# A two-layer trunk on one core: the opening's order on VectorE written anew up to the fourth k-tile, and two rows of set 2 given to TensorE

## The chip, the core and the metric

The kernel runs on one core of one Trainium2 chip. The metric is device time in microseconds (us) of one execution; lower is better. Times are medians of several runs. The profile is of one execution of its own.

## The reference

The input is x (512 rows of 2048, float32) and a conditioning vector c (2048). Two layers follow each other; each has its own modulation by c. What matters here is only the beginning of the first layer:

```python
c_act = jax.nn.silu(c)
mod = c_act @ w_mod[l] + b_mod[l]
shift, scale, gate = jnp.split(mod, 3, axis=-1)
h = x * (1.0 + scale[:, None]) + shift[:, None]
proj = h @ w_in            # q, k, v and a gate of the first layer's attention
```

So no product `h @ w_in` can begin before a part of shift and scale is known, and each of these is a product of c_act with a 2048 x 2048 part of w_mod. After that come differential attention, an output product, a layer norm, a shared key/value product, forgetting attention, a second output product and a last layer norm.

## The kernel before

**Precision.** Every large product is done as three TensorE products (lines 174 to 176): each operand is split into a high part (`whi`, `hh`) and a low remainder (`wlo`, `hl`). A weights' split is a copy on ScalarE (L94, `whi`) and a subtraction on VectorE (L95, `wlo`). A split step loads two k-tiles of a job; the first job of a head is 384 wide, the second 512 (768 and 1024 numbers per partition).

**The opening** (from L439) works in k-tiles of 128 of the 2048 model columns. For k-tile `kt` it needs:

- the *set* that holds the k-tile's shift and scale. Sets 0 and 1 hold one k-tile each, the others two (set 2 holds k-tiles 2 and 3). A set is summed over 16 rows (pieces of 128 of the reduction). A row is one VectorE instruction: the first row writes `sacc` (L496), the 15 others add to it (L498). The pieces arrive as tiles `sms` (L471), in a ring of 5 buffers (`NBUF`);
- the *sums* of the set (`mod_sums`, L512): TensorE multiplies `sacc` with a column of ones (L528) into the bank `tr`. For set 1 TensorE also takes the last 8 of the 16 rows by itself, straight from `sms` and the column of c_act (L525, `on_pe`, L449);
- the *columns* (`mod_columns`, L531; `mcol` on VectorE, L534): the sums plus the bias;
- the *turn* (`turn_x`, L536): four transposes of x on TensorE (L539) into the same bank `tr`, of which there is one buffer; two ScalarE instructions read it with the columns, `hh` (L543) and `htmp` (L544);
- the *lower h* (`lower_h`, L548, `hl` on VectorE), which needs `htmp`;
- the *products* of the k-tile (`first_products`): 21 matmuls (7 accumulators, three products each) of 128x512 into the banks `sc` (2), `o` (1) and `acc` (4).

Products run in phases for two heads u: head 0 with k-tiles 0 to 3, then head 1 with 0 to 7, head 0 with 4 to 11, and so on. After head 0's fourth k-tile the accumulators are copied out by ScalarE (`part`, L576).

**What sets the order.** The string `START` (L31) is the order in which these steps are recorded: `c` sums, `m` columns, `t` turn, `l` lower h, `s` the next weights' split, `g` the products of the next k-tile, and a digit n for n rows of `sacc` (`dv`). Within `with tc.manual_schedule(engines={ET.DVE})` VectorE's queue stands exactly in that order; the queues of TensorE and ScalarE are ordered by a scheduler when the program is built. `sums()` first empties the set (`dv(-1)`). The rows come from a generator (`mod_steps`), which yields after it has recorded a row; so when `dv(-1)` stops, the first row of the next set has already been recorded, ahead of the columns of the set just summed.

Of the kernel before, what the change touches and what calls it, by code (L numbers as in the profile page):

```python
# [10 lines left out]
F32 = mybir.dt.float32  # L11
# [5 lines left out]
P = 128  # L17
D = 2048
KT = D // P
# [8 lines left out]
ET = mybir.EngineType  # L28


START = "cmtlssg6c6t1lgcst4g3tsl9sggts8sl6s2gtggts7lgsstlgg2s7gstl2ss9gsgtslgg5stgg6lsstg2gss8sggt2g4l4sgstctslggtslssggssgggg"  # L31
LAM_INIT = 0.8 - 0.6 * math.exp(-0.0)


# [76 lines left out]
def tile_yoco(  # L111
# [44 lines left out]
    def acc_bank(name="acc"):  # L156
        return ps.tile([P, 512], F32, name=name, tag="acc", bufs=4)
# [281 lines left out]
    with tc.tile_pool(name="start", bufs=2, reuse_waits="tile") as sp, tc.manual_schedule(engines={ET.DVE}):  # L439
# [7 lines left out]
            nc.sync.dma_start(xts[q][:, :, f0:f1], src.rearrange("(b p) f -> p b f", p=P))  # L447

        def on_pe(i):  # L449
            return 8 if i == 1 else 0  # L450


        tiles = []
# [8 lines left out]
        def load_mods(upto):  # L462
            while state["next"] < min(upto, len(tiles)):
                i, k, nr = tiles[state["next"]]
                k0, nk = sets[i]
                t = sp.tile([P, nr, 2, nk * P], F32, name="sms", tag="sms", bufs=NBUF)
                step = nr // 2 if i < 2 else nr
                for kq in range(0, nr, step):
                    for v in range(2):
                        rows = w_mod[0, (k + kq) * P : (k + kq + step) * P, v * D + k0 * P : v * D + (k0 + nk) * P]  # L470
                        nc.sync.dma_start(t[:, kq : kq + step, v, :], rows.rearrange("(k p) n -> p k n", p=P))  # L471
                loaded[i, k] = t
                state["next"] += 1
                if k == 0:
                    if k0 == 0:
                        load_x(0, 0, P)
                    elif k0 == 1:
                        load_x(0, P, T)
                    elif k0 % 4 == 0:
                        load_x(k0 // 4, 0, T)  # L480

        accs = {}

        def mod_steps():
            for n, (i, k, nr) in enumerate(tiles):
                k0, nk = sets[i]
                load_mods(n + NBUF)
                if k >= KT - on_pe(i):
                    continue
                if k == 0:  # L490
                    accs[i] = sp.tile([P, 2, 2 * P], F32, name="sacc", tag="sacc", bufs=2)
                acc = accs[i][:, :, : nk * P]
                for kq in range(nr):
                    w, sc = loaded[i, k][:, kq, :, :], cact[:, k + kq : k + kq + 1]
                    if k + kq == 0:
                        V.tensor_scalar(acc, w, sc, None, op0=ALU.mult)  # L496
                    else:
                        V.scalar_tensor_tensor(acc, w, sc, acc, op0=ALU.mult, op1=ALU.add)  # L498
                    yield i

        load_mods(2)
        ws.load(2)
        steps = mod_steps()
        ahead = [next(steps)]

# [6 lines left out]
        def mod_sums(i):  # L512
            k0, nk = sets[i]
            nr = 8 // nk
            dv(-1)
            state["set"] = i + 1
            load_mods(max(n for n, t in enumerate(tiles) if t[0] == i) + 1)
            pm = tr_bank()
            for v in range(2):
                for j in range(nk):  # L520
                    js = slice(j * P, (j + 1) * P)
                    dst = pm[:, nk * v + j : nk * v + j + 1]
                    for k in range(KT - on_pe(i), KT):
                        kr = k // nr * nr
                        PE.matmul(  # L525
                            dst, loaded[i, kr][:, k - kr, v, js], cact[:, k : k + 1], start=k == KT - on_pe(i), stop=False
                        )
                    PE.matmul(dst, accs[i][:, v, js], ones[:, 0:1], start=on_pe(i) == 0, stop=True)  # L528
            return pm
# [20 lines left out]
        acc = {}  # L550
# [71 lines left out]

        for tok in START:
            if tok.isdigit():
# [473 lines left out]
    acc = [acc_bank() for _ in range(TB)]  # L1098
# [313 lines left out]
```

## Time and profile before

| what | us |
|---|---|
| median of 3 runs (1977.61 to 1982.32) | 1979.31 |
| the profiled execution's own time | 1977.16 |
| its span on the core | 1975.4 |
| TensorE matmul busy | 1938.9 |
| VectorE busy | 1342.1 |
| ScalarE busy | 704.8 |
| first product of the opening (L174) | 18.17 |
| first product of k-tiles 1, 2 and 3 | 33.05, 43.52, 50.24 |

A row of the timeline gives start, duration, engine, line, operation, output <- inputs, shapes and count; in square brackets stands the idle time of the engine just before it and what ended it. A row of the waits gives total, number and longest. A row of the windows gives, for a stretch, the busy time of each engine, then the granted TensorE clock (1.00 is full), the share of the DMA engines and GB/s. One fp32 matmul of one column (L525, L528) stands as two records.

### The profile page before, as it was taken

The page shows a single profiled execution, that of the slowest core. Times are in us where ns is not written, and L with a number is a line of the kernel's source. Part 1 is how long each engine was busy: PE and PEld are TensorE (multiplying, and loading weights), DVE is VectorE, ACT ScalarE, POOL GpSimd, SP SyncE. Part 2 cuts the span into 40 slices and gives each one's busy share as a digit, 9 for nine tenths or more (in the row PEclk, how much of TensorE's full clock was granted, in tenths as well). Part 3 has the DMA queues.
Part 4 walks back from the last instruction along what each step waited for, and adds up shares of the span by engine and source line. Part 5 has one row for each costly group of instructions (what it writes and reads, how often), then busy time and mean ns, then how long its engine had stood idle before and what let it go on. Part 6 is the DMA issues. An engine that isn't in the chain of part 4 may idle for free.

```text
span 1975.4 us, 25112 instructions
## 1 busy us (share of the span) xinstructions
PE 1938.9 (98%) x8939; PEld 1605.5 (81%) x8939; DVE 1342.1 (68%) x2460; ACT 704.8 (36%) x1217; POOL 2.2 (0%) x10
## 2 busy tenths in 40 slices
PE   5999999999999999999999999999999999999997
PEld 4888888888888888788888888888888888888886
DVE  7885677778777777863475665666466666676657
ACT  2432445333333334431264222224343443453123
POOL 0000000000000000000000000000000000000000
PEclk8999999999999999999999999999999999999999
DMA  9993444676667666553345765664355555553622
GB/s 343 355 310 106 134 149 152 192 223 194 221 193 223 198 219 216 195 159 98 115 160 182 267 232 183 222 221 144 102 152 151 155 156 153 148 173 114 229 90 107
DMA packets 299354, 362.21 MB, mean 183 GB/s; under 512 B 44598, under 2 KB 201932, under 8 KB 298460
## 3 DMA queue, kind: packets, MB, share of 16 engines
q1 hardware_dynamic: 296848, 356.39, 56.4%
q10 hardware_dynamic: 2380, 4.21, 0.6%
q8 instruction: 70, 1.15, 0.2%
q14 instruction: 56, 0.46, 0.1%
HBM read 338.68 MB, written 21.84 MB: 183 GB/s over the span
## 4 chain that ended last, share of the span: by engine, by line
PE 93%; DVE 3%; DMA 2%; SPq 1%; issue 0%; ACT 0%; DVEq 0%; ACTq 0%
PE acc L174 27%; PE acc L175 27%; PE acc L176 27%; PE sc L174 2%; PE sc L175 2%; PE sc L176 2%; PE o L174 1%; PE o L175 1%; PE o L176 1%; DVE wlo L95 1%; SPq L471 0%; PE tr L742 0%; PE tr L789 0%; PE tr L539 0%; DMA nr<-n_dram 0%
## 5 line engine op out<-in xcount | busy, mean ns | idle before, releaser
L95 DVE TENSOR_TENSOR wlo<-wst,whi 128x1024 fp32r<-128x1024 f32 (+2 forms) x322 | 384.3, 1195 | 332.6 <-ACT whi L94 323.2
L94 ACT CAST whi<-wst 128x1024 fp32r<-128x1024 f32 (+2 forms) x322 | 331.7, 1031 | 693.4 <-PE acc L176 345.4
L174 PE MATMUL acc<-whi,hh 128*128 128x512 f32 x1232 | 484.1, 396 | 2.3 <-DVE sg L695 1.2
L175 PE MATMUL acc<-wlo,hh 128*128 128x512 f32 x1232 | 480.8, 390 | 0.1
L176 PE MATMUL acc<-whi,hl 128*128 128x512 f32 x1232 | 480.4, 390 | 0.0
L174 PE MATMUL acc<-hh,whi 128*128 128x512 f32 x1184 | 465.5, 393 | 0.1
L175 PE MATMUL acc<-hl,whi 128*128 128x512 f32 x1184 | 461.9, 390 | 0.0
L176 PE MATMUL acc<-hh,wlo 128*128 128x512 f32 x1184 | 460.8, 390 | 0.0
L174 PEld LDWEIGHTS acc<-whi,hh 128*128 128x128 f32 x1232 | 232.4, 189 | 49.0 <-DVE ztmp L926 1.5
L176 PEld LDWEIGHTS acc<-whi,hl 128*128 128x128 f32 x1232 | 231.3, 188 | 49.5
L175 PEld LDWEIGHTS acc<-wlo,hh 128*128 128x128 f32 x1232 | 231.6, 188 | 45.3 <-DVE wlo L95 0.6
L176 PEld LDWEIGHTS acc<-hh,wlo 128*128 128x128 f32 x1184 | 222.3, 188 | 47.7
L174 PEld LDWEIGHTS acc<-hh,whi 128*128 128x128 f32 x1184 | 222.5, 188 | 44.0 <-issue 1.4
L175 PEld LDWEIGHTS acc<-hl,whi 128*128 128x128 f32 x1184 | 222.6, 188 | 41.7
L391 DVE SCALAR_TENSOR_TENSOR macc<-ms,cact,macc 128x512 f32<-128x512 f32 x300 | 224.2, 747 | 36.0 <-DMA ms<-in_kv_w_mod_dram 21.4
L498 DVE SCALAR_TENSOR_TENSOR sacc<-sms,cact,sacc 128x512 f32<-128x512 f32 (+1 forms) x127 | 89.5, 705 | 5.3 <-DMA sms<-in_w_mod_dram 1.6
L725 ACT ACTIVATE e<-e,mn 128x128 f32<-128x128 f32 (+3 forms) x64 | 36.0, 563 | 121.0 <-DVE mn L721 120.8
L1218 ACT ACTIVATE eb<-eb,mnb 128x128 f32<-128x128 f32 (+1 forms) x64 | 36.0, 563 | 88.7 <-DVE mnb L1215 88.5
L1215 DVE CUSTOM_DVE_ANT_0 eb<-sc,biasb 128x128 f32<-128x128 f32 (+1 forms) x64 | 31.0, 485 | 22.1 <-PE sc L176 21.4
L391 DVE SCALAR_TENSOR_TENSOR macc<-msk,cact,macc 128x512 f32<-128x512 f32 x60 | 45.0, 750 | 1.4
L721 DVE CUSTOM_DVE_ANT_0 e<-sc,bias 128x128 f32<-128x128 f32 (+3 forms) x64 | 31.0, 485 | 16.4 <-PE sc L176 16.4
L791 ACT ACTIVATE ogT<-tr,subg 128x128 f32<-128x128 f32 x64 | 20.0, 363 | 46.1 <-PE tr L789 46.0
(263 smaller groups left out, 1768.6 us busy)
## 6 DMA issues: line engine op xcount, KB each, us to landing
wst<-in_a_w_in_dram SPq DMA_DIRECT2D x240, 256.0 KB, 3.8
ms<-in_w_mod_dram SPq DMA_DIRECT2D x64, 512.0 KB, 4.4
ms<-in_kv_w_mod_dram SPq DMA_DIRECT2D x64, 512.0 KB, 4.3
wst<-in_kv_w_dram SPq DMA_DIRECT2D x64, 512.0 KB, 3.8
wst<-in_b_w_in_dram SPq DMA_DIRECT2D x128, 256.0 KB, 3.0
sms<-in_w_mod_dram SPq DMA_DIRECT2D x56, 512.0 KB, 6.8
wst<-in_a_w_out_dram SPq DMA_DIRECT2D x32, 512.0 KB, 3.7
msk<-in_w_mod_dram SPq DMA_DIRECT2D x64, 256.0 KB, 5.6
```

What stands on the lines that cost most here:

```text
L94: self.nc.scalar.copy(hi[:, :, :w], st[:, :, :w])
L95: self.nc.vector.tensor_tensor(lo[:, :, :w], st[:, :, :w], hi[:, :, :w].bitcast(F32), op=ALU.subtract)
L174: PE.matmul(dst, lhs[0], rhs[0], start=start, stop=False)
L175: PE.matmul(dst, lhs[0], rhs[1], start=False, stop=False)
L176: PE.matmul(dst, lhs[1], rhs[0], start=False, stop=stop)
L391: ins = V.scalar_tensor_tensor(acc, w, cact[:, kt : kt + 1], acc, op0=ALU.mult, op1=ALU.add)
L498: V.scalar_tensor_tensor(acc, w, sc, acc, op0=ALU.mult, op1=ALU.add)
L721: V.tensor_tensor_reduce(out=e[:, :w], in0=sc[:, :w], in1=st["bias"][:, (3 - i) * P :], scale=-1.0, scalar=3.0e38, op0=ALU.add, op1=ALU.mi ...
L725: S.activation(e[:, :w], e[:, :w], AF.Exp, bias=mn, scale=-1.0, accum_out=rs)
L791: S.activation(ogT[2 * h + e][:, i * P : (i + 1) * P], pt[:, e * P : (e + 1) * P], AF.Copy, scale=subg[:, e : e + 1])
L1215: V.tensor_tensor_reduce(out=e[:, :w], in0=sc[:, :w], in1=bias[:, :w], scale=-1.0, scalar=3.0e38, op0=ALU.add, op1=ALU.min, accum_out=mn)
L1218: S.activation(e[:, :w], e[:, :w], AF.Exp, bias=mn, scale=-1.0, accum_out=rs)
```

## The change

Four things change, all in the opening.

1. `START` is written anew up to the fourth k-tile.
2. `mod_steps` yields before it records a row instead of after it. `dv(-1)` then stops ahead of the next set's first row, and the columns of a set are recorded ahead of that row, in all sets.
3. TensorE takes 2 rows of set 2 (L526 in the changed file, one line later than before), VectorE 14 instead of 16.
4. Through the new string one weights' split (768 numbers) stands ahead of the last rows of set 2 instead of behind them.

```diff
-START = "cmtlssg6c6t1lgcst4g3tsl9sggts8sl6s2gtggts7lgsstlgg2s7gstl2ss9gsgt...
+START = "cmt4lssgc4t3lsgcmt2lgtls9s5ggts8sl6s2gtggts7lgsstlgg2s7gstl2ss9gsgt...
```

```diff
         def on_pe(i):
-            return 8 if i == 1 else 0
+            return {1: 8, 2: 2}.get(i, 0)
...
                 load_mods(n + NBUF)
-                if k >= KT - on_pe(i):
-                    continue
-                if k == 0:
-                    accs[i] = sp.tile([P, 2, 2 * P], F32, name="sacc", tag="sacc", bufs=2)
-                acc = accs[i][:, :, : nk * P]
                 for kq in range(nr):
+                    if k + kq >= KT - on_pe(i):
+                        break
+
+                    yield i
+                    if k + kq == 0:
+                        accs[i] = sp.tile([P, 2, 2 * P], F32, name="sacc", tag="sacc", bufs=2)
+                    acc = accs[i][:, :, : nk * P]
                     w, sc = loaded[i, k][:, kq, :, :], cact[:, k + kq : k + kq + 1]
...
                         V.scalar_tensor_tensor(acc, w, sc, acc, op0=ALU.mult, op1=ALU.add)
-                    yield i
```

The rest of both strings is the same. Up to the fourth k-tile the changed program's queues, as built, stand so (names as in the profile; `x` counts equal instructions):

```
VectorE, after the 16 rows of set 0:
mcol | 4 rows of set 1 | hl (kt 0) | wlo 768 | wlo 1024 | 4 rows of set 1
4 rows of set 2 | mcol | 3 rows | hl (kt 1) | wlo 768 | 7 rows of set 2
mcol | 2 rows of set 3 | hl (kt 2) | wlo 1024 | hl (kt 3) | wlo 768
9 rows of set 3 | wlo 1024 | 5 rows of set 3 | mcol | wlo 768 | 8 rows of set 4 | wlo 1024 | hl

TensorE, from the 21 products of kt 1 on:
L526 tr<-cact,sms x2 | L529 tr<-ones,sacc      (four times)
L540 tr<-ident,xt x4 (kt 2) | 7 products of hh and whi (kt 2)
L540 tr<-ident,xt x1 (kt 3) | the other 14 products of kt 2
L540 tr<-ident,xt x3 (kt 3) | 21 products of kt 3
```

In the program before, all four transposes of kt 3 stand between the 7 and the 14 products of kt 2. ScalarE's queue has `hh` and `htmp` of kt 1 ahead of the weights' copy (L94) that stood ahead of them. On SyncE the first 43 transfers of the opening keep their order; behind them a pair of weights' loads moves ahead of six `sms` transfers. GpSimd's queue is unchanged. From the last products of the opening on, the order on TensorE is that of before, instruction for instruction.

More of the change, by code (lines that the diff above doesn't have):

```diff
@@ L28 @@
 ET = mybir.EngineType
-START = "cmtlssg6c6t1lgcst4g3tsl9sggts8sl6s2gtggts7lgsstlgg2s7gstl2ss9gsgtslgg5stgg6lsstg2gss8sggt2g4l4sgstctslggtslssggssgggg"
+START = "cmt4lssgc4t3lsgcmt2lgtls9s5ggts8sl6s2gtggts7lgsstlgg2s7gstl2ss9gsgtslgg5stgg6lsstg2gss8sggt2g4l4sgstctslggtslssggssgggg"
 LAM_INIT = 0.8 - 0.6 * math.exp(-0.0)
```

## Prediction

> **What bounds the kernel now.** First the page's busy times and its chain of waits:
>
> ```profile
> PE 1938.9 (98%) x8939; PEld 1605.5 (81%) x8939; DVE 1342.1 (68%) x2460; ACT 704.8 (36%) x1217; POOL 2.2 (0%) x10
> ...
> PE 93%; DVE 3%; DMA 2%; SPq 1%; issue 0%; ACT 0%; DVEq 0%; ACTq 0%
> ```
>
> Then the waits of TensorE from 50 us to the end:
>
> ```profile
> PE acc L174 <- DVE sg L695: 1.2, 2, 0.6
> PE acc L174 <- DVE ztmp L926: 1.1, 1, 1.1
> PE sc L984 <- DVE n L997: 0.7, 1, 0.7
> PE tr L789 <- DVE og L775: 0.5, 1, 0.5
> ```
>
> TensorE is busy 98% of the span, and behind 50 us it waits 3.5 us in all, each time for VectorE work that itself follows a product. Nothing there would absorb a shift: a us that TensorE loses or wins in the opening is a us at the end. So I read the opening alone, for TensorE's idle time, in the timeline:
>
> ```profile
> 14.57 0.98 PE L528 MATMUL tr<-ones,sacc 128*128 128x1 f32 x4 [11.17 <-DVE sacc L498]
> 15.71 0.35 DVE L496 TENSOR_SCALAR sacc<-sms,cact 128x256 f32<-128x256 f32 x1 [1.28 <-DMA sms<-in_w_mod_dram]
> 15.97 0.15 DVE L534 TENSOR_TENSOR mcol<-tr,bcol 128x2 f32<-128x2 f32 x1
> ...
> 25.09 1.84 PE L525 MATMUL tr<-cact,sms 128*128 128x1 f32 x16
> 25.54 4.69 DVE L498 SCALAR_TENSOR_TENSOR sacc<-sms,cact,sacc 128x512 f32<-128x512 f32 x6
> 28.80 0.36 PE L528 MATMUL tr<-ones,sacc 128*128 128x1 f32 x2
> 30.14 0.15 DVE L534 TENSOR_TENSOR mcol<-tr,bcol 128x2 f32<-128x2 f32 x1
> 30.35 1.11 PE L539 MATMUL tr<-ident,xt 128*128 128x128 f32 x4 [1.19 <-DVE mcol L534]
> 31.49 0.83 ACT L94 CAST whi<-wst 128x768 fp32r<-128x768 f32 x1 [12.70 <-DMA wst<-in_a_w_in_dram]
> 32.23 0.77 ACT L543 ACTIVATE hh<-tr,mcol 128x512 fp32r<-128x512 f32 x1
> 33.05 1.22 PE L174 MATMUL sc<-hh,whi 128*128 128x512 f32 x2 [1.59 <-ACT hh L543]
> 33.70 0.69 DVE L548 TENSOR_TENSOR hl<-htmp,hh 128x512 fp32r<-128x512 f32 x1 [2.69 <-ACT htmp L544]
> 34.31 6.26 DVE L498 SCALAR_TENSOR_TENSOR sacc<-sms,cact,sacc 128x512 f32<-128x512 f32 x8
> 40.71 1.02 PE L528 MATMUL tr<-ones,sacc 128*128 128x1 f32 x8 [1.16 <-DVE sacc L498]
> 41.77 0.16 DVE L534 TENSOR_TENSOR mcol<-tr,bcol 128x4 f32<-128x4 f32 x1
> 41.99 0.66 PE L539 MATMUL tr<-ident,xt 128*128 128x128 f32 x4 [0.26 <-DVE mcol L534]
> 42.69 0.78 ACT L543 ACTIVATE hh<-tr,mcol 128x512 fp32r<-128x512 f32 x1 [2.22 <-PE tr L539]
> 43.52 1.22 PE L174 MATMUL sc<-hh,whi 128*128 128x512 f32 x2 [0.87 <-ACT hh L543]
> ```
>
> From 30 us on TensorE idles 1.19 + 1.59 + 1.16 + 0.26 + 0.87 = 5.1 us: that is all that a better order can win there, besides the clock. The columns of k-tile 1 (30.14) wait behind six rows (to 30.23), although their sums end at 29.16. `hl` idles 2.69 us for `htmp`, and the eight rows behind it start only after it: VectorE takes its queue in order.
>
> **The changed steps up to k-tile 2.**
>
> *Columns ahead of the waiting row.* The first sums end at 15.55; the columns came at 15.97, behind a row that waited for a transfer. Now they follow the sums: -0.4.
>
> *Columns of set 1.* Four rows stand ahead of them instead of six and one. They start at about 29.2 less what is left of the 0.4: about -1.0.
>
> *`hh` ahead of the weights' copy on ScalarE.* The transposes ended at 31.46, `hh` began at 32.23 behind a copy of 0.83: -0.75. Together k-tile 1's products start about 2 us sooner, near 31.1.
>
> *Set 2's sums.* `hl` of k-tile 1 can start at 31.8 instead of 33.70, but now a split of 768 stands ahead of the last rows, and it needs its copy, which ScalarE does only after `htmp`: the split runs from about 32.8 to 33.7. Seven rows of 6.26/8 = 0.783 follow, to 39.2; before, the last row ended at 34.31 + 6.26 = 40.57. That leaves 1.35 of the lead. TensorE gives it back: 2 rows for 4 columns are 8 more matmuls, at 1.84/8 = 0.23 each (the row of 25.09 has two records per matmul), and only the first 2 stand ahead of the first wait. Behind it come 6 x 0.23 + 4 x 0.25 = 2.4 us against the 1.02 of 40.71. So the sums end at 41.6 against 41.73, and k-tile 2's products start at 43.5, as before. I take 0 here; the ends are -1.4 (these matmuls hidden) and +0.5 (all 8 behind the wait).
>
> **K-tile 3 and what follows.** VectorE and TensorE of before in this stretch:
>
> ```profile
> 41.85 2.32 DVE L498 SCALAR_TENSOR_TENSOR sacc<-sms,cact,sacc 128x512 f32<-128x512 f32 x3
> 45.00 0.75 DVE L498 SCALAR_TENSOR_TENSOR sacc<-sms,cact,sacc 128x512 f32<-128x512 f32 x1 [0.83 <-DMA sms<-in_w_mod_dram]
> 46.27 1.22 DVE L95 TENSOR_TENSOR wlo<-wst,whi 128x1024 fp32r<-128x1024 f32 x1
> 46.57 0.60 PE L539 MATMUL tr<-ident,xt 128*128 128x128 f32 x4
> 47.40 2.33 DVE L498 SCALAR_TENSOR_TENSOR sacc<-sms,cact,sacc 128x512 f32<-128x512 f32 x3
> 49.64 0.95 DVE L95 TENSOR_TENSOR wlo<-wst,whi 128x768 fp32r<-128x768 f32 x1
> 50.24 0.61 PE L174 MATMUL sc<-hh,whi 128*128 128x512 f32 x2
> 50.51 0.69 DVE L548 TENSOR_TENSOR hl<-htmp,hh 128x512 fp32r<-128x512 f32 x1
> 51.11 6.26 DVE L498 SCALAR_TENSOR_TENSOR sacc<-sms,cact,sacc 128x512 f32<-128x512 f32 x8
> ```
>
> Before, `hh` of k-tile 3 was made under the 14 remaining products of k-tile 2 (46.9 to 50.2), and VectorE did eight rows of set 3 ahead of `hl` of k-tile 3 (one at 40.48, then 3 + 1 + 3). Now one transpose stands ahead of the 14 products and three behind them. They end near 50.25; `hh` takes 0.78 and the hand-over some 0.1, with nothing else in TensorE's queue: k-tile 3's products start at 51.15. That is **+0.9**.
>
> The larger cost lies on VectorE. Ahead of `hl` of k-tile 3 it has only two rows, `hl` and a split, and is through at 46.4. Then it waits for `htmp` until 51.8, over 5 us, with 14 rows of set 3 queued behind (before: 8 left at 51.1). This backlog I follow with 0.2275 per product (14 in 3.2), 0.78 per row, 1.13 and 0.87 from start to start for splits of 1024 and 768:
>
> - `hl` 0.6, split 0.87, 9 rows 7.0: the split of head 1's second job runs from 60.3 to 61.5. TensorE wants it after 43 products, 51.15 + 9.8 = 60.9: **+0.6**.
> - 5 rows to 65.3; TensorE needs 17 products and four sums, to 66.3. Columns, split, first row, 7 rows, split of 1024: to 74.5. TensorE: 25 products, 8 transposes, 73.05: **+1.4**.
> - `hl`, 6 rows, split of 768: 80.65, against 80.4 after 26 products; then 2 rows ahead of the sums and the columns behind: four small waits, **+0.65**.
> - Set 4's turns now come when TensorE has few products left to put between: the second waits for the one bank `tr` (0.6), the next products for a copy behind `htmp` (0.45), then for its split (0.35): **+1.4**.
> - `hl` of k-tile 6: split from 86.4, first row, 6 rows, `hl` to 93.35; TensorE wants it at 92.4: **+0.9**.
>
> After that VectorE has caught up. **The sum**: 0 + 0.9 + 0.6 + 1.4 + 0.65 + 1.4 + 0.9 = **+5.85**, say +5.8. Against the profiled execution's 1977.16 that is 1983.0; this execution lies 2.15 below the median of 1979.31, so I forecast **1985.1** for a median.
>
> **The transfers and the other queues.** The early split moves a pair of weights' loads ahead of six `sms` transfers on SyncE.
>
> ```profile
> 28.80:32.20 3.40, 1.47 (x8) 0.99 (x7) 2.17 (x4) 0.71 (x1) 0.00 (x0) 0.58 1.10 380
> 42.50:45.90 3.40, 2.53 (x8) 1.90 (x7) 2.50 (x5) 1.45 (x2) 0.00 (x0) 0.58 1.09 380
> 45.90:60.00 14.10, 14.10 (x69) 11.77 (x68) 12.85 (x19) 6.74 (x11) 0.00 (x0) 0.98 1.09 384
> ```
>
> The transfers run at 384 GB/s, so those six come 0.5 MB / 384 = 1.4 us later. VectorE reaches them over 4 us later than before: nothing, by that cover, and 1.4 if VectorE were not late. GpSimd does nothing here.
>
> **The clock.** These rows also show the granted clock at 0.58 around the starts of k-tiles 1 and 2, so seven products take 0.425 instead of 0.227. I leave the second stretch as it is, since TensorE waits and does one-column matmuls ahead of it in both programs. [...]
>
> **The rivals.**
>
> *A. The forecast*, +4 to +7.5: 0.66 (a little of it below 4).
>
> *B. The backlog is absorbed.* VectorE idles 0.93 and 2.82 us for sums near 59 and 77 us:
>
> ```profile
> 59.84 0.16 DVE L534 TENSOR_TENSOR mcol<-tr,bcol 128x4 f32<-128x4 f32 x1 [0.93 <-PE tr L528]
> 78.77 0.16 DVE L534 TENSOR_TENSOR mcol<-tr,bcol 128x4 f32<-128x4 f32 x1 [2.82 <-PE tr L528]
> ```
>
> If TensorE's order left it enough products at each late split, only the +0.9 and one or two of the smaller waits would stay: +0.9 to +2.5. Against it: both idle stretches are waits for sums that themselves come later. 0.15.
>
> *C. The whole delay reaches TensorE.* Six more rows (4.7), a split (0.9) and `hl` 1.3 later make 6.9, with 0.9 in front: +7.5 to +9. 0.09.
>
> *D. The clock stays up at 42.5*, because one-column matmuls fill more of the stretch ahead: 7 x 0.2 = 1.4 less, +4.4. 0.05. [...]
>
> *E. Faster.* The lead of 2 us survives to k-tile 2 and the clock stays up: of the 5.1 us idle the three hand-overs (0.87 + 0.87 + 0.26) remain, 3.1 go, with 1.4 of clock: -4.5. It decides at `hl` of k-tile 3: VectorE must have work until `htmp`, or wait there without being late at the splits after 60 us. Its queue has two rows there, which speaks against it. 0.05.
>
> That the order changes as said is plain from the built queues.
>
> **How the numbers follow.** About 0.2% (4 us) is what a measurement of this kernel can tell from no change. Slower by more: most of A, C and most of D, 0.75. Within: B and the lower edges of A and D, 0.20. Faster: E, 0.05. The range reaches from B's lower end (+0.9, 1980.2) to C's upper end (+9.2, 1988.5).
>
> **What would show it.** Right: k-tile 1's first product near 31, k-tile 2's near 43.5; an idle stretch near 51 ended by `hh` on ScalarE; `hl` of k-tile 3 with over 5 us idle ahead of it; five to ten idle stretches of TensorE between 60 and 95 us, ended by `wlo`, `hl` or `hh`, 4 to 6 us in all. Wrong: no wait of TensorE behind 55 us (B or E), or k-tile 2 starting before 42.5 (the added matmuls hidden).

## The result and the profile after

The changed kernel takes **1984.6 us** (median of 8 runs, 1982.99 to 1986.09); the kernel before 1979.37 (8 runs, 1976.24 to 1982.32). The ratio is 1.0025, with a 95% interval of 1.0014 to 1.0035: slower, by 5.2 us between the medians. The profiled execution took 1983.33 us with a span of 1981.5, so 6.2 us more than the profiled one of before.

The page first, busy times and the chain of waits:

```profile
PE 1944.5 (98%) x8955; PEld 1607.7 (81%) x8955; DVE 1341.3 (68%) x2458; ACT 704.5 (36%) x1217; POOL 2.2 (0%) x10
...
PE 89%; DVE 6%; DMA 3%; issue 1%; SPq 1%; ACT 1%; DVEq 0%; ACTq 0%
```

TensorE has 16 more records (eight matmuls of two records), VectorE two instructions less. The chain's shares moved by more than the change can account for: TensorE's went from 93% to 89%, and 4% of the span is 79 us. Among the lines that came into the chain are `macc` (L391) and its transfers, which belong to a later part of the program, so I read nothing from the shares. TensorE's waits from 50 us to the end say more:

```profile
PE acc L174 <- DVE sg L696: 1.8, 3, 0.6
PE acc L175 <- DVE wlo L95: 1.6, 2, 1.3
PE sc L174 <- ACT hh L544: 0.9, 1, 0.9
...
PE sc L175 <- DVE hl L549: 0.7, 1, 0.7
...
PE tr L540 <- ACT htmp L545: 0.4, 1, 0.4
PE acc L174 <- ACT whi L94: 0.3, 1, 0.3
```

The waits for `sg` are old (they lie far behind the opening). Those for `wlo`, `hh`, `hl`, `htmp` and `whi` are new; all lie between 51 and 95 us. The timeline of TensorE shows them one by one, and the starts of the k-tiles:

```profile
29.51 0.69 PE L540 MATMUL tr<-ident,xt 128*128 128x128 f32 x4 [0.26 <-DVE mcol L535]
31.07 1.22 PE L174 MATMUL sc<-hh,whi 128*128 128x512 f32 x2 [0.87 <-ACT hh L544]
39.45 0.38 PE L529 MATMUL tr<-ones,sacc 128*128 128x1 f32 x2 [0.29 <-DVE sacc L500]
42.10 0.66 PE L540 MATMUL tr<-ident,xt 128*128 128x128 f32 x4 [0.26 <-DVE mcol L535]
43.62 1.21 PE L174 MATMUL sc<-hh,whi 128*128 128x512 f32 x2 [0.87 <-ACT hh L544]
51.61 0.73 PE L174 MATMUL sc<-hh,whi 128*128 128x512 f32 x2 [0.87 <-ACT hh L544]
61.27 0.39 PE L176 MATMUL o<-hh,wlo 128*128 128x512 f32 x1
61.98 0.50 PE L175 MATMUL acc<-wlo,hh 128*128 128x512 f32 x1 [0.32 <-DVE wlo L95]
62.31 0.39 PE L176 MATMUL acc<-whi,hl 128*128 128x512 f32 x1
73.42 0.39 PE L176 MATMUL o<-hh,wlo 128*128 128x512 f32 x1
75.13 0.50 PE L175 MATMUL acc<-wlo,hh 128*128 128x512 f32 x1 [1.33 <-DVE wlo L95]
86.22 0.66 PE L540 MATMUL tr<-ident,xt 128*128 128x128 f32 x4 [0.38 <-ACT htmp L545]
93.06 0.39 PE L174 MATMUL sc<-hh,whi 128*128 128x512 f32 x1
94.14 0.50 PE L175 MATMUL sc<-hl,whi 128*128 128x512 f32 x1 [0.69 <-DVE hl L549]
```

K-tile 1 starts 2 us sooner than before (31.07 against 33.05), k-tile 2 at the same time (43.62 against 43.52), k-tile 3 1.4 later (51.61 against 50.24). Read the pair at 73.42 and 75.13: products in a row start 0.23 us apart, these two 1.71. The wait costs 1.5 us, while the row lists 1.33 of idle time: the record of the matmul before it lasts 0.39 us, 0.16 more than the 0.23 between starts, and covers the rest. That is so at each wait (61.27 to 61.98: 0.48 for a listed 0.32), so waits are measured here from start to start. The step behind a wait is longer too (61.98 to 62.31: 0.33 instead of 0.23) and is counted with it.

VectorE in the same stretch:

```profile
33.92 5.47 DVE L500 SCALAR_TENSOR_TENSOR sacc<-sms,cact,sacc 128x512 f32<-128x512 f32 x7
41.88 0.16 DVE L535 TENSOR_TENSOR mcol<-tr,bcol 128x4 f32<-128x4 f32 x1 [2.49 <-PE tr L529]
...
44.88 1.22 DVE L95 TENSOR_TENSOR wlo<-wst,whi 128x1024 fp32r<-128x1024 f32 x1
52.26 0.69 DVE L549 TENSOR_TENSOR hl<-htmp,hh 128x512 fp32r<-128x512 f32 x1 [6.16 <-ACT htmp L545]
52.87 0.95 DVE L95 TENSOR_TENSOR wlo<-wst,whi 128x768 fp32r<-128x768 f32 x1
53.74 7.05 DVE L500 SCALAR_TENSOR_TENSOR sacc<-sms,cact,sacc 128x512 f32<-128x512 f32 x9
60.71 1.22 DVE L95 TENSOR_TENSOR wlo<-wst,whi 128x1024 fp32r<-128x1024 f32 x1
```

VectorE stands still for 6.16 us ahead of `hl` of k-tile 3, with nine rows and a split behind it. The split of 60.71 is the one that TensorE waits for at 61.98.

The starts of the same products, counted in order of time, give the sum (the first row is k-tile 2's first product, the second k-tile 3's):

| product no. | before | after | later by |
|---|---|---|---|
| 43 | 43.52 | 43.62 | 0.10 |
| 64 | 50.24 | 51.61 | 1.37 |
| 127 | 66.32 | 68.01 | 1.69 |
| 169 | 75.97 | 79.80 | 3.83 |
| 221 | 89.65 | 96.33 | 6.68 |
| 1001 | 272.46 | 279.18 | 6.72 |
| 7001 | 1630.29 | 1636.81 | 6.52 |
| end of the span | 1975.37 | 1981.55 | 6.18 |

Behind 97 us nothing more is lost, and 0.5 us is won back. The loss lies in the stretch from k-tile 2's first product to product 221.

### The profile page after: what moved, and what is told of

It is laid out like the page before. It is cut to its first block, busy times and chain, and to the rows that moved or that the text cites. A ratio compares the mean times of both kernels' runs of the same rounds, so it can differ in the third digit from the quotient of the medians.

```text
span 1981.5 us, 25144 instructions
## 1 busy us (share of the span) xinstructions
PE 1944.5 (98%) x8955; PEld 1607.7 (81%) x8955; DVE 1341.3 (68%) x2458; ACT 704.5 (36%) x1217; POOL 2.2 (0%) x10
## 4 chain that ended last, share of the span: by engine, by line
PE 89%; DVE 6%; DMA 3%; issue 1%; SPq 1%; ACT 1%; DVEq 0%; ACTq 0%
PE acc L174 26%; PE acc L175 26%; PE acc L176 26%; PE sc L174 2%; PE sc L175 2%; PE sc L176 2%; PE o L174 1%; PE o L175 1%; PE o L176 1%; DVE sacc L500 1%; DVE wlo L95 1%; DMA ms<-in_w_mod_dram 1%; DVE macc L391 1%; DMA ms<-in_kv_w_mod_dram 1%; DMA xt<-in_x_dram 1%
## 5 line engine op out<-in xcount | busy, mean ns | idle before, releaser
L94 ACT CAST whi<-wst 128x1024 fp32r<-128x1024 f32 (+2 forms) x322 | 331.6, 1031 | 674.4 <-PE acc L176 333.8
L391 DVE SCALAR_TENSOR_TENSOR macc<-ms,cact,macc 128x512 f32<-128x512 f32 x300 | 224.3, 748 | 37.4 <-DMA ms<-in_kv_w_mod_dram 21.0
L1216 DVE CUSTOM_DVE_ANT_0 eb<-sc,biasb 128x128 f32<-128x128 f32 (+1 forms) x64 | 31.1, 485 | 22.5 <-PE sc L176 21.9
L391 DVE SCALAR_TENSOR_TENSOR macc<-msk,cact,macc 128x512 f32<-128x512 f32 x60 | 45.0, 750 | 1.4
```

Of the source, the lines that this page charges most:

```text
L94: self.nc.scalar.copy(hi[:, :, :w], st[:, :, :w])
L391: ins = V.scalar_tensor_tensor(acc, w, cact[:, kt : kt + 1], acc, op0=ALU.mult, op1=ALU.add)
L1216: V.tensor_tensor_reduce(out=e[:, :w], in0=sc[:, :w], in1=bias[:, :w], scale=-1.0, scalar=3.0e38, op0=ALU.add, op1=ALU.min, accum_out=mn)
```

## The experiments

Seven kernels, in two series of runs (the first four versions, then the last three). The kernel before had a median of 1978.40 (30 runs) in the first and 1978.86 (25 runs) in the second; ratios are against those. A profile is one execution, and executions of one kernel spread over 2 to 6 us, so the places of the waits are read from the profiles and the worth of an edit from the ratios.

The theory to be tested (W): ahead of `hl` of k-tile 3 VectorE has only two rows of set 3; it waits there for `htmp`, and the 14 rows behind it make the later splits late. The rivals: the eight added matmuls of set 2 are the loss (M); the columns put ahead of a set's first row in every set are (C). These letters are not those of the prediction's rivals.

**The old order, with the other edits kept.**

```diff
-START = "cmt4lssgc4t3lsgcmt2lgtls9s5ggts8s...
+START = "cmtlssg6c6t1lgcst4g3tsl9sggts8s...
```

> The string of before, with both other edits (columns ahead of the next set's first row; two rows of set 2 on TensorE). Theory W (the loss is VectorE waiting for k-tile 3's htmp with two rows ahead of it, and the late splits behind): seven rows stand ahead of that lower h again, so no idle of VectorE over 1 us near 50, no wait of TensorE behind 45 us over 0.3; 1979.0 to 1980.5, k-tile 2's products at 43.5 to 44.5. Theory M (the loss is the eight added matmuls of set 2): they are still here, so some 2 us stay: 1981 to 1982.5, and k-tile 2's products come 1.4 us later than in the kernel before. Theory C (the loss is the columns put ahead in every set): 1983 to 1985, as in the changed kernel.

1979.7 us (11 runs), ratio 1.0004 [0.9996, 1.0013]: no difference from before that can be measured, although TensorE still takes two rows of set 2 and the columns stand ahead of the first rows. TensorE has no wait for `wlo`, `hl` or `hh` behind k-tile 2 in its trace. VectorE around k-tile 3:

```profile
47.55 2.32 DVE L500 SCALAR_TENSOR_TENSOR sacc<-sms,cact,sacc 128x512 f32<-128x512 f32 x3
49.79 0.95 DVE L95 TENSOR_TENSOR wlo<-wst,whi 128x768 fp32r<-128x768 f32 x1
50.66 0.69 DVE L549 TENSOR_TENSOR hl<-htmp,hh 128x512 fp32r<-128x512 f32 x1
```

`hl` follows without idle time: rows cover the wait for `htmp`. This speaks against M and C as causes of the whole loss, and for the order. One thing came as M had it and not as W had it: k-tile 2's first product.

```profile
44.78 1.22 PE L174 MATMUL sc<-hh,whi 128*128 128x512 f32 x2 [0.87 <-ACT hh L544]
```

That is 1.26 us later than before (43.52), where W had 43.5 to 44.5: in the old order the added matmuls do cost at k-tile 2. The ratio's interval leaves room for a loss of that size (up to 2.6 us), but not for 5.

**The new order, TensorE's two rows given back to VectorE.**

```diff
-            return {1: 8, 2: 2}.get(i, 0)
+            return {1: 8}.get(i, 0)
```

> The changed kernel without the two rows of set 2 on TensorE: VectorE takes all 16. Theory W: the two rows cost VectorE 1.6 us ahead of the sums and the sums take 1.0 instead of 2.4, so k-tile 2's products start within 0.4 us of the changed kernel's 43.6; the idle of VectorE near 50 us (over 5 us) stays, and so do the waits for wlo near 62 and 75 us; 1982.0 to 1984.6, depending on what the scheduler makes of the order after 80 us. Theory M: k-tile 2's products start at 42.0 and the total is 1982.5 or below with the waits unchanged. Theory C: 1984.6.

1983.2 us (8 runs), ratio 1.0026 [1.0015, 1.0036]: as slow as the changed kernel. M falls as the cause of the loss: it had at most 1982.5, and k-tile 2 at 42.0. TensorE at k-tile 2:

```profile
41.13 1.41 PE L529 MATMUL tr<-ones,sacc 128*128 128x1 f32 x8 [3.43 <-DVE sacc L500]
...
44.78 1.22 PE L174 MATMUL sc<-hh,whi 128*128 128x512 f32 x2 [0.87 <-ACT hh L544]
```

The start of k-tile 2, which I had expected within some tenths of the changed kernel's 43.62, comes 1.2 us later. Most of that is the clock, which fell sooner in this profile (at 41.60, under the sums): the sums took 1.41 us instead of the 1.02 that the same eight records took before, and the transposes 1.11 instead of 0.66. The rows by themselves account for some 0.3: VectorE's two rows (1.6) against the six matmuls behind the wait (1.4). At the end no difference from the changed kernel is left to be measured.

**Seven rows ahead of `hl` of k-tile 3 instead of none.** Only rows of set 3 move across `hl` and a split:

```diff
-START = "cmt4lssgc4t3lsgcmt2lgtls9s5ggts8s...
+START = "cmt4lssgc4t3lsgcmt2lgt7ls2s5ggts8s...
```

> The changed kernel with seven of the rows that stood behind k-tile 3's lower h put ahead of it; nothing else in the string moves. Theory W: VectorE's idle near 50 us falls from 6.2 to under 2; the split that came late near 62 is in time, that near 75 nearly; TensorE's start-to-start loss from 60 to 100 us falls from 5.3 to about 1.5; the wait of 0.9 for hh near 51.6 stays, since TensorE's transposes stand as in the changed kernel; 1980.5 to 1981.8. Theories M and C: 1984.6, nothing that they name is touched.

1980.9 us (11 runs), ratio 1.0014 [1.0005, 1.0022]. Against 1.0025 [1.0014, 1.0035] about half of the loss is gone by the medians, by a move of seven rows and nothing else on VectorE. The intervals still overlap, but the runs do not: the slowest of these eleven took 1982.56, and of the sixteen of the changed kernel and of the version before this one (measured in the same series) only one took less, 1982.49. VectorE ahead of `hl`, then TensorE's waits from 50 us on:

```profile
51.87 0.69 DVE L549 TENSOR_TENSOR hl<-htmp,hh 128x512 fp32r<-128x512 f32 x1 [0.76 <-ACT htmp L545]
```

```profile
PE sc L174 <- ACT hh L544: 0.9, 1, 0.9
PE tr L529 <- DVE sacc L500: 0.7, 1, 0.7
...
PE acc L175 <- DVE wlo L95: 0.2, 1, 0.2
```

VectorE idles 0.76 us ahead of `hl` instead of 6.16, and TensorE's waits have the splits down from 1.6 to 0.2; a new one of 0.7 is for the sums of set 3, whose rows now end last. TensorE's order, which the build's scheduler sets, differs too behind k-tile 3's first products, so the move is not perfectly alone. W holds; the idle time ahead of `hl` is not all of the loss.

**The new order up to k-tile 1, the old one behind it.**

```diff
-START = "cmt4lssgc4t3lsgcmt2lgtls9s5ggts8s...
+START = "cmt4lssgc4t3lsgcst4g3tsl9sggts8s...
```

> The string of the changed kernel up to the sums of set 2, then that of before (split, turn, 4 rows, products, 3 rows, turn, split, lower h, 9 rows). Theory W: k-tile 1's products at 31 and k-tile 2's near 43 as in the changed kernel, seven rows ahead of k-tile 3's lower h as before; one wait for hh near 51 (all four transposes stand behind k-tile 2's products), none over 0.3 after it; 1979.5 to 1980.8. Theory M: 1981.5 to 1982.5. Theory C: 1984.

1979.32 us (11 runs), ratio 1.0005 [0.9996, 1.0014]. With the old order from k-tile 2 on nothing of the loss can be measured any more. Nothing is gained either, although k-tile 1 starts 1.9 us sooner than before:

```profile
31.15 1.22 PE L174 MATMUL sc<-hh,whi 128*128 128x512 f32 x2 [0.87 <-ACT hh L544]
41.65 0.66 PE L540 MATMUL tr<-ident,xt 128*128 128x128 f32 x4 [0.26 <-DVE mcol L535]
43.18 0.91 PE L174 MATMUL sc<-hh,whi 128*128 128x512 f32 x2 [0.87 <-ACT hh L544]
51.19 0.73 PE L174 MATMUL sc<-hh,whi 128*128 128x512 f32 x2 [0.87 <-ACT hh L544]
```

K-tile 2 is 0.3 sooner than before, k-tile 3 0.95 later: the hand-over to `hh` at 51.19 (all four transposes stand behind k-tile 2's products, then ScalarE makes `hh`, then TensorE goes on) is the forecast's +0.9 by itself. VectorE idles ahead of `hl` here too:

```profile
51.84 0.69 DVE L549 TENSOR_TENSOR hl<-htmp,hh 128x512 fp32r<-128x512 f32 x1 [3.05 <-ACT htmp L545]
```

Nine rows of set 3 stand behind it, and TensorE waits for no split. So 3 us of idle time with nine rows left make no split late; 6 us with fourteen do.

**The kernels side by side.** These are the starts of the same products in each profile, in us later than in the kernel before, and how long the granted clock was at half in the opening after its first rise (10.24 us in the kernel before):

| kernel | no. 43 (k-tile 2) | no. 64 (k-tile 3) | no. 221 | lost from 64 to 221 | half clock |
|---|---|---|---|---|---|
| changed | 0.11 | 1.37 | 6.68 | 5.31 | 10.24 |
| old order | 1.27 | 2.56 | 2.57 | 0.01 | 13.65 |
| no rows on TensorE | 1.26 | 2.62 | 5.48 | 2.86 | 13.65 |
| seven rows ahead | -0.27 | 0.98 | 2.81 | 1.83 | 10.24 |
| mixed order | -0.34 | 0.95 | 1.45 | 0.50 | 10.24 |

The late splits lie between 64 and 221. The loss there is nothing with the old order, small with the mixed one, and largest in the two kernels that have only two rows of set 3 ahead of `hl`. Between those two it differs (5.31 and 2.86); the build's scheduler ordered TensorE's products otherwise in places, and why the second loses less there is not shown. What is lost up to k-tile 3 is another matter: it is there in the old order too, and by estimate 3.41 us more of half clock are worth some 1.6 us of products (0.43 us each instead of 0.23). Whether that extra stretch belongs to a kernel or to the one execution that was profiled is not shown.

**Where k-tile 1's lead goes.** The lead of 2 us falls into a stretch of half clock (in the mixed order the windows give 0.50 from 30 to 33 us, 0.51 from 33 to 36.8 and 1.00 behind). Three kernels on the mixed order put 128x512 matmuls of zero weights (they add zero to open accumulators) behind the columns' sums, to ask what the clock answers to:

```diff
+    nil = const.tile([P, P], F32R, name="nil")
+    S.activation(nil, ident, AF.Copy, scale=0.0)
...
                     PE.matmul(dst, accs[i][:, v, js], ones[:, 0:1], start=on_pe(i) == 0, stop=True)
+                    for b in range({1: 3}.get(i, 0)):
+                        PE.matmul(acc[0][b % 4], nil, Hh[0], start=False, stop=False)
```

The lines are those of the first, with three behind each of set 1's two columns; the second has `{1: 6}`, the third `{1: 3, 2: 2}`.

> The mixed order (columns and set 1 as in the changed kernel, everything behind k-tile 1 as before) with six more 128x512 matmuls of zero weights on TensorE, three behind each column's sums of set 1; they add zero to open accumulators. It asks why the two microseconds that k-tile 1 gains are lost again at the half clock. Theory K: the clock falls because the 6.8 us ahead of k-tile 1 hold too few full-width products (some 2.1 us of them in the mixed order; 3.5 us here, about half). Then the granted clock stays 1.0 or falls later than 30 us, k-tile 1's first product comes at about 32.5 (6 x 0.23 = 1.4 later) and its 21 products take under 6 us instead of 7.5. The time is then between 0.5 below and 1 us above the mixed order's 1979.3, since VectorE's rows of set 2, started behind hl, come 1.4 later. Theory N: what TensorE does in that stretch does not matter; the clock falls near 30 for 6.8 us as before, k-tile 1 takes 7 us or more, and the time is 1 to 2 us above the mixed order's.

1981.31 us (10 runs), ratio 1.0015 [1.0005, 1.0024]. The clock fell all the same, at 29.21 for 6.83 us: with six, the forecast of theory K (too few full-width products make the clock fall) failed, and the time is in the range of theory N (what TensorE does there does not matter).

> As the run with six zero-weight matmuls, with twelve (six behind each column's sums of set 1). Theory K: if half of the 6.8 us was too little, 4.8 us of full-width products in them (70%) is enough: the clock does not fall near 30, k-tile 1's first product comes at about 33.9 (2.7 later than in the mixed order) and its 21 products take under 5.5 us. The time is 1 to 2.5 us above the mixed order's. Theory N: the clock falls all the same, k-tile 1 takes 7 us, the time is 2.5 to 4 us above the mixed order's.

1982.26 us (10 runs), ratio 1.0018 [1.0008, 1.0027]. With twelve the clock did not fall there. The windows of this kernel, in pieces of 3.41 us (the shortest stretch at half clock that these openings show, as in the changed kernel from 43.67 to 47.08):

```profile
27.29:30.71 3.42, 3.42 (x27) 3.15 (x26) 0.43 (x1) 0.00 (x0) 0.00 (x0) 1.00 1.09 380
30.71:34.12 3.41, 2.54 (x14) 1.94 (x15) 2.37 (x4) 1.21 (x2) 0.00 (x0) 1.00 1.10 380
34.12:37.53 3.41, 3.41 (x17) 2.80 (x16) 3.07 (x4) 1.65 (x3) 0.00 (x0) 1.00 1.10 388
37.53:40.95 3.42, 1.61 (x10) 1.33 (x8) 3.25 (x5) 1.20 (x2) 0.00 (x0) 1.00 1.05 390
40.95:44.36 3.41, 2.85 (x14) 2.85 (x14) 1.65 (x2) 0.00 (x0) 0.00 (x0) 0.50 1.08 385
44.36:47.78 3.42, 2.69 (x12) 2.21 (x12) 1.73 (x4) 0.43 (x1) 0.00 (x0) 0.50 1.09 386
47.78:51.19 3.41, 3.01 (x7) 2.43 (x8) 3.30 (x6) 1.02 (x2) 0.00 (x0) 0.50 1.09 385
```

The granted clock (the third number from the end) stays 1.00 up to 40.95. K-tile 1's 21 products take 4.9 us, from 33.74 to 38.64, against 7.5 in the mixed order (31.15 to 38.66): 2.6 us less, for twelve matmuls of 0.23 (2.7) ahead. But `hl` of k-tile 1 came later with them, and behind it the rows of set 2: TensorE waited 2.4 us for `sacc`, and the clock fell at 40.95 instead. It stayed at half for 10.24 us, as long as the two stretches of the mixed order together (6.83 and 3.41): the half clock was moved, not shortened. The time is 2.9 us above the mixed order's, over K's 1 to 2.5 (the kernel before took 0.5 more in the second series of runs than in the first).

> As the run with six zero-weight matmuls ahead of k-tile 1, and eight more ahead of k-tile 2 (two behind each of the four columns' sums of set 2). Theory K: the second fall of the clock (43.6 in the mixed order, for 3.4 us) goes as well or comes later, and k-tile 2's first nine products take 0.23 us each instead of 0.43 (1.7 less), against 8 x 0.23 = 1.8 more ahead of them: the time is that of the run with six, within 1 us. Theory N: both falls stay, and the time is 1.5 to 2.5 us above the run with six.

1982.22 us (10 runs), ratio 1.0018 [1.0009, 1.0028]. The clock fell twice, at 30.62 and at 44.28, for 6.83 us each: K's forecast of the clock failed here too, while the time is 0.9 above the run with six, as K had it. The build's scheduler had put all eight matmuls of set 2 ahead of its sums, from 40.06 to 41.92, so that the last 3.41 us ahead of the second fall held only 1.05 us of them.

Side by side, these are the 128x512 products in the 3.41 us ahead of a fall: 0 us in the changed kernel ahead of 30.02, 0.78 with six zero-weight matmuls ahead of 29.21, 1.22 and 1.05 with fourteen ahead of 30.62 and 44.28, 1.11 with twelve ahead of 40.95 (each matmul is counted up to the start of the next). With twelve, the window from 27.29 to 30.71 held 1.48 us of them, and the clock was 1.00 behind it. One-column matmuls did not hold it up in the changed kernel. These are its windows ahead of its first fall and behind it,

```profile
26.60:30.02 3.42, 3.17 (x28) 2.99 (x28) 2.60 (x5) 0.00 (x0) 0.00 (x0) 1.00 1.09 385
30.02:33.43 3.41, 2.54 (x8) 1.88 (x7) 2.70 (x5) 2.28 (x3) 0.00 (x0) 0.50 1.10 376
```

where TensorE is busy for 3.17 of 3.42 us, with one-column matmuls and transposes alone, and the clock is 0.50 right behind. So N falls with the run of twelve, where the added matmuls were all that changed and the clock did not fall near 30. K's forecast of the clock held there and failed with six and with fourteen. Each of these points is one profile, and what in such a stretch decides is not shown.

No version tried beats the kernel before; the old order with the other edits kept (1.0004) and the mixed order (1.0005) come nearest.

## Why the prediction was right, point by point

**K-tile 1: right.** Forecast near 31.1, measured 31.07; columns ahead of a waiting row, fewer rows ahead of set 1's columns and `hh` ahead of the copy gave about what their rows promised (columns at 29.29 instead of 30.14, no copy ahead of `hh`). These two come to 1.6 of the 2.0. The other 0.4 was not in the forecast's terms, though its "about 2" covers it: the four transposes took 0.69 us (29.51) instead of 1.11, since the clock was still at full until 30.02.

**K-tile 2 unchanged: right.** Set 2's rows were forecast to end at 39.2 and ended at 39.39 (33.92 + 5.47), the sums at 41.6 and ended just ahead of `mcol` at 41.88; the first product was forecast at 43.5 and came at 43.62. Two of the eight added matmuls stand ahead of the wait and six behind it, as forecast. In the run without them k-tile 2 came 1.2 later, but some 0.8 of that is the clock.

**K-tile 3: right in kind, too small.** Forecast +0.9, measured +1.37. The hand-over is there (0.87 idle ahead of 51.61, in the trace of the mixed order as well). Of the other 0.47, 0.1 is the later start of k-tile 2, and by estimate some 0.2 is the half clock (half a microsecond more of it, with 0.43 us a product instead of 0.23), which began at 43.67, right at k-tile 2's first product, and lasted until 47.08; before it had begun at 43.03 and ended at 46.44, so k-tile 2 had only 2.92 us of it. Where the stretch falls differs from profile to profile, so this part may be chance. The rest is the transposes: the forecast had them end near 50.25, where they only began (50.26); they end at 50.75.

**The backlog on VectorE: right.** Forecast over 5 us idle ahead of `hl`, measured 6.16. The late splits came where they were counted. From start to start, less what the same steps take without a wait, and with the longer step behind each wait:

| term | forecast | measured |
|---|---|---|
| hand-over at k-tile 3, with the clock | 0.9 | 1.48 |
| split of head 1's second job, 61.98 | 0.6 | 0.59 |
| split of 1024, 75.13 | 1.4 | 1.60 |
| four small waits, 69 to 84 us | 0.65 | 0.57 |
| set 4's turns, 86 to 89 us | 1.4 | 1.48 |
| `hl` of k-tile 6, 94.14 | 0.9 | 0.96 |
| sum | 5.85 | 6.68 |

The measured sum is the 6.68 of product no. 221. Most of what the forecast missed is the hand-over, the rest nearly all the split of 1024.

By the profiled executions the change is 6.17 (1983.33 against 1977.16), since 0.5 is won back later, by the medians 5.2 (2.8 to 6.9 by the ratio's interval). That the forecast of 5.8 lies between the two is in part luck: its terms are 0.8 short of the opening's loss, and the 0.5 won back was not in it.

Seven rows moved ahead of `hl` took away about half of the ratio's excess (and 3.5 of the 5.3 us lost between k-tile 3 and product 221), and with the old order behind k-tile 1 none of it can be measured: the cause of the late splits was shown by moving it, not only read. The transfers that moved are no rival: the mixed order keeps the early split, and no row of VectorE between 40 and 99 us of the changed kernel waits for a transfer.

**The rivals.** B (absorbed) fell: there was no slack at the splits. C (all 6.9 us reach TensorE) fell, if not by much: 5.2 of them did in the profile, behind the hand-over. (C's upper end is +9 in the list of rivals and +9.2 in the range; nothing hangs on it.) D (the clock stays up at 42.5) fell: it was half from 43.67 to 47.08. The changed kernel's row from 26.60 to 30.02 speaks against D's reason too: TensorE was busy for 3.17 of 3.42 us with one-column matmuls and transposes, and the clock was 0.50 right behind.

E (faster) needed work for VectorE ahead of `hl` of k-tile 3 and the clock up, and had neither. The mixed order, which puts seven rows there, is no faster than before either. Two things stand against k-tile 1's lead. With the clock at half up to 36.8 its 21 products take 7.5 us, instead of the 4.9 that they take at full clock in the run with twelve: they end at 38.66, 0.7 ahead of before, from a start 1.9 ahead. And set 2's rows end at 38.87 (33.40 + 5.47) however fast these products are.

**What was argued too loosely.** I costed the lead at k-tile 1 by VectorE's rows alone. By estimate, TensorE at full clock (31.07 + 4.9, the 4.9 from the run with twelve) would have come to set 2's sums at about 36 and waited for `sacc` until 39.4 all the same, so the 0 stands, and the clock alone is not what keeps the lead from k-tile 2; but it is the reason why the lead shows as no wait (0.29 us at 39.45).

Open is how much of the spread between executions of one kernel comes from where the stretches of half clock lie: products went from 0.43 to 0.23 us apart at 22.39 in one profile (with six zero-weight matmuls) and at 23.88 in another (with twelve). No run was made for it.

## What to carry to other kernels

VectorE took its queue in order here: nine rows stood behind `hl` of k-tile 3 and began at 53.74, after `hl` at 52.26. Such a queue needs enough independent work ahead of an instruction that waits for a far hand-over: with two rows ahead of it VectorE stood still for 6 us and five later operands came late; seven rows moved ahead of it took about half of the loss away. Before an edit brings a stage forward, look at which resource the stage then lands on: of two microseconds won at k-tile 1, 1.2 were spent at half clock, and the bound at the next stage was another engine's rows in any case. Where an engine's records overlap, as TensorE's do here (0.39 us long, 0.23 apart), measure a wait from start to start; the listed idle time here was short by some 0.15 us each time, and the step behind the wait was 0.1 longer than usual.

## What the runs showed of the hardware

In these openings TensorE's granted clock did not follow its busy time. In the changed kernel it fell to 0.50 right behind 3.42 us in which TensorE was busy for 3.17 with one-column float32 matmuls and 128x128 transposes, and with twelve zero-weight matmuls it stayed at 1.00 behind 3.41 us in which TensorE was busy for 2.54 (30.71 to 34.12). It also stayed at 1.00 behind the window from 27.29 to 30.71 of that run, with 1.48 us of 128x512 products in it, their weights zero. Six such matmuls did not do it: three of them lay in the stretch ahead of the fall (0.78 us), three behind it. With twelve the clock fell later, at 40.95, after TensorE had waited 2.4 us for rows that they had made late, and stayed at half for 10.24 us, as long as in the mixed order's two stretches together. The first rise of the clock came at another time in each profile: 23.19 us in the changed kernel, 22.39 with six, 23.88 with twelve.
